# A hybrid DeltaNet layer on one core: reloads, squares and stores placed elsewhere in the queues, weight pairs dealt 18 and 14

## The chip, the cores and the metric

The kernel runs on one core of one Trainium2 chip. Its time is device microseconds of one execution; lower is better. Engines: TensorE (PE, with PEld for its weight loads), VectorE (DVE), ScalarE (ACT), GpSimd (POOL), and SyncE (SP), which only issues DMAs. ScalarE can issue DMAs too. Each engine works through its own list of instructions in order: an instruction that waits holds up all behind it.

## The reference

One layer on x of 2048 steps by 1024 features, all float32:

```python
h = rmsnorm(x, norm_in_w)
proj = h @ w_in            # 1024 -> 8208 columns
qkv, z_g, b_g, a_g, gate_b, gate_c, h_c, z_c = split(proj)
qkv = silu(causal_depthwise_conv(qkv, conv_qkv_w))      # 4 taps
o = gated_delta_rule_chunked(l2norm(q)/sqrt(128), l2norm(k), v, g, beta)   # 8 heads, state 128x128
o = rmsnorm(o, gdn_norm_w) * silu(z_g)
y_c = gate_b * (causal_depthwise_conv(gate_c * h_c, conv_w) + conv_b) * silu(z_c)   # 3 taps
return rmsnorm(x + concat(o, y_c) @ w_out, final_norm_w)
```

## The kernel before, in words

**Precision.** Every large product is done in float16 with both operands split in a high and a low part: three matmuls (high by high, high by low, low by high) stand for one. On top of that the input projection uses Strassen's scheme: two blocks of 512 steps against two blocks of 128 columns take 7 products instead of 8. So a *pair* of column blocks for one half of the steps (1024) is 7 products of 12 matmuls of 128 by 512, that is 84 matmuls `ps_d<-xop,g` (or `gr`).

**Pairs and stages.** There are 32 pairs of column blocks: `kq` and `vz` for each of 8 heads, `ca` and `cb` for each of 8 channel groups. Each is needed for both halves of the steps, 64 in all. `PLAN` (L26) deals them to four *stages*, four heads each: stage A has heads 0 to 3 on the first half, B the same on the second half, C heads 4 to 7 on the first half, D the same on the second. Entry (n, m) of a head puts n conv pairs between its `kq` and its `vz`, and m behind. Before, every stage has 16 pairs. Then comes stage E, the output projection. By the count of the matmuls, pair 0 starts at 32.4 us of the span, pair 1 at 104.9, stage B at 539.1, C at 991.3, D at 1403.6, E at 1780.6.

**Weights.** A pair's float32 columns come in two DMAs of 512 KB (`raw`, issued by SP, `fetcher`). `scales` squares both on ScalarE (`junk_sq<-raw`, 1.04 us each) to find a power of two as scale, `prepare_hi` makes the high parts on ScalarE (`g<-raw`, `g<-st`), `prepare_lo` the low ones on VectorE. Five results per pair (tags G1, G2, G7, G3, G4, one buffer each in stage A) are stored to DRAM (`wc<-g`, 512 or 256 KB); a buffer is written again only after its store has read it. In stage A the products read the `g` tiles at once, while the pairs of set one (`NA_` of them, 16) are split; in stages B and C set two is split meanwhile, and stages B, C and D load the split weights back (`gr<-wc`, SP). `raw` buffers: four in stage A, two later.

**Operands from x.** Seven tiles of 1 MB (`xop`) hold the split Strassen operands of one half; at the end of each stage they are loaded anew from `x0d` or `x1d` (`reload_x`, issued by ScalarE), each as soon as its last product of the stage is done. `later_x` makes `x1d` during stage A.

**Heads.** `gdn` runs beside the pairs: chunk matrices, an inversion on GpSimd (`nbx`, 31 steps), then a recurrence over 8 chunks, each a chain TensorE, VectorE, TensorE, ScalarE (`u<-ps_r`), TensorE, VectorE.

**Order.** All of these are Python generators. While the program is built, a model clock (`Clock`) gives every instruction a cost, and `do` hands an instruction out when the model says that its inputs are `lead` us away or past: 0 for ScalarE and VectorE, -2 for SP, `SAFE` = -4 for the squares (so, ready 4 us ago). A smaller number thus puts an instruction later in its queue, behind more work of its engine. The chip follows the order, not the model's times. On the chip every DMA, from whichever queue, uses one of 8 completion semaphores in turn, and the queue that issues it waits until the DMA eight places before it has landed (`DMAHW` in the built program).

**Evacuation.** ScalarE copies five of a pair's results out of PSUM (`c<-ps_d`); the products have four PSUM banks, so TensorE soon waits when ScalarE stands still.

Of the kernel before, what the change touches and what calls it, by code (L numbers as in the profile page):

```python
# [24 lines left out]
SAFE = -4.0  # L25
RATE = {"SP": 330e3, "ACT": 200e3}  # L26
PLAN = (((4, 0), (2, 0), (1, 0), (1, 0)), ((2, 0),) * 4, ((2, 0),) * 4, ((1, 0), (1, 0), (1, 1), (0, 4)))
# [204 lines left out]
def hybrid_layer_kernel(ctx, tc, x, norm_in_w, w_in, conv_qkv_w, A_log, dt_bias, gdn_norm_w,  # L232
# [10 lines left out]
    KT = KD // 2  # L243
# [189 lines left out]
    HH, GG = H // 2, G // 2  # L433
    for qt in range(4):
        grp, half = divmod(qt, 2)
        convs = [(f, half, grp * GG + g) for g in range(GG) for f in ("ca", "cb")]
        n0 = len(pairs)
        for i in range(HH):
            h = grp * HH + i
            order.append((half, h))  # L440
            pair("kq", half, h)
            if grp == 0 and i == 0:
                plan.append(("gates", half, 0, None))
            n, m = PLAN[qt][i]
            for c in convs[:n]:
                pair(*c)
            pair("vz", half, h)
            for c in convs[n:n + m]:
                pair(*c)
            convs = convs[n + m:]  # L450
        QOF += [qt] * (len(pairs) - n0)
        for p in range(n0, len(pairs)):
            if half == 0:
                WID.append(len(prep))
                prep.append(p)
            else:
                WID.append(WID[pairs.index((0,) + pairs[p][1:])])
# [155 lines left out]
    def first_x():  # L613
# [14 lines left out]
        def block0():  # L628
            for k in range(KD):
                pt = yield from acq("t")  # L630
                yield from trans(pt, k, 0)
                o = xop[X11 if k < KT else X21]
                yield from do(ACT.activation, kept(k), pt, AF.Copy, scale=sx_of(k))
                rel(pt)
                yield from split16(o[:, k % KT], kept(k))
                mark("x", 0, X11 if k < KT else X21, k % KT)

        def block1():
            for i in range(CB, 2 * CB):
                yield from norm_tile(xt0[i], junk[:, i % 2])  # L640
            for kt in range(KT):
# [6 lines left out]
                rel(pt)  # L648
                pt = yield from acq("t")
# [69 lines left out]
    def reload_x():  # L719
        yield from need(("x0d",))  # L720
        for qt in range(1, 4):
            for o in PRODUCTS:
                yield from need(("free", qt - 1, o))
                src = x1d[STORED.index(o)] if qt % 2 else x0d[o]
                xop[o] = hp.tile([P, KT, NR, 2, QW], F16, tag=f"X{o}", name="xop")
                yield from do(ACT.dma_start, xop[o].rearrange("p k r s w -> p (k r s w)"),
                              src.rearrange("p k r s w -> p (k r s w)"))
                for kt in range(KT):
                    mark("x", qt, o, kt)
# [10 lines left out]
    def scales():  # L740
        for p in range(NP):
# [5 lines left out]
            for j in range(2):  # L747
                yield from do(ACT.activation, junk_sq, raws[p, j].rearrange("p k c -> p (k c)"),
                              AF.Square, accum_out=ss[:, j:j + 1], lead=SAFE if p else None)
            pt = yield from acq("t")  # L750
            yield from do(PE.matmul, pt[:, 0:2], ones_b, ss.bitcast(BF16)[:, 1::2], start=True, stop=True,
                          lead=-3.0 if p else None)
# [30 lines left out]
    def prepare_lo():  # L783
        def keep(g, at, p, tag):
# [3 lines left out]
            yield from do((ACT if p < NA_ else SP).dma_start, wcd[p][:, at * WG:at * WG + n], g.rearrange("p s k c -> p (s k c)"))  # L788
# [356 lines left out]
    def gdn(half, h, st):  # L1145
# [160 lines left out]
        for b in range(2):  # L1306
            po = yield from acq("o")
            po = po.rearrange("p (c i) -> p c i", i=P)
            for i in range(CB):
# [7 lines left out]
                else:  # L1317
                    yield from do(PE.matmul, pa, kq(c)[:, 0, :], S, start=True, stop=True)
                    yield from do(DVE.scalar_tensor_tensor, r, pa, dec[:, 0, h, c:c + 1], vp[:, c, :],
                                  op0=ALU.mult, op1=ALU.subtract, back=9.0)  # L1320
                    yield from do(PE.matmul, po[:, i, :], S, kq(c)[:, 1, :], start=True, stop=False)
                yield from do(PE.matmul, pu, W[:, c, :], r, start=True, stop=True)
                u = sm.tile([P, P], F32, tag="u", name="u")
                yield from do(ACT.activation, u, pu, AF.Copy, back=9.0)
                yield from do(PE.matmul, pe, ksts[b][:, i, :], u, start=True, stop=True)
# [5 lines left out]
                yield from do(PE.matmul, po[:, i, :], u, NA(c)[:, 1, :], start=first, stop=True)  # L1331
# [251 lines left out]
    spawn(later_x(), 2)  # L1583
# [104 lines left out]
```

## Time and profile before

| | before |
|---|---|
| median of 3 runs | 2143.87 us (2138.94 to 2148.57) |
| the profiled execution | 2136.86 us, span 2135.1 us |
| mean granted TensorE clock | 0.957 of 2.4 GHz |
| TensorE busy | 1937.4 us, 91% |
| VectorE, ScalarE, GpSimd busy | 61%, 45%, 42% |

An engine's busy time is the union of its instructions. The clock is given as a share of the full 2.4 GHz; its lower level here is 0.5 (1.2 GHz). A time in brackets behind a row of the timeline is the idle time of that engine just before, with what ended it.

### The profile page before, as it was taken

To read this page: it belongs to the slowest core of one execution; us is meant where nothing else is said; L and a number is where in the kernel's file an instruction comes from. 1 tells how busy PE (TensorE), PEld (TensorE's weight loads), DVE (VectorE), ACT (ScalarE), POOL (GpSimd) and SP (SyncE) were. 2 spreads that over 40 slices of the span, in tenths; PEclk is the share of its full clock that TensorE was granted. 3 is DMA by queue.
4 is the path that set the end of the run, shared out by engine and by line. 5 is a ranking of instruction groups with operands and counts; after the bars stand their busy time and mean duration, and the time that the engine had idled before them with its cause. 6 is when DMAs were issued, how large, how long until landed. Compare 5 with 4: busy or idle time off the path is not lost. (4 is left out here: it accounts for less than half of the span.)

```text
span 2135.1 us, 30331 instructions
## 1 busy us (share of the span) xinstructions
PE 1937.4 (91%) x10832; PEld 1055.9 (49%) x10832; DVE 1307.1 (61%) x2437; ACT 968.5 (45%) x1884; POOL 899.5 (42%) x1441
## 2 busy tenths in 40 slices
PE   3696898787999989887999999999999999999998
PEld 1343354345555545444555555546656555444443
DVE  5785777866786656564758676655675754523321
ACT  5564565544554444343545555354544534423210
POOL 3446533745547373634463737245546261100000
PEclk9798899898999999998999999899999999999999
DMA  6357676775766786758676766585656668423110
GB/s 152 83 116 177 184 178 172 191 199 173 217 142 196 128 181 139 175 146 284 171 193 155 208 188 178 188 282 169 196 170 205 193 209 318 141 92 112 66 49 30
DMA packets 262381, 360.37 MB, mean 169 GB/s; under 512 B 67661, under 2 KB 180694, under 8 KB 258646
## 3 DMA queue, kind: packets, MB, share of 16 engines
q1 hardware_dynamic: 246678, 299.71, 53.3%
q10 hardware_dynamic: 15552, 58.73, 7.3%
q8 instruction: 85, 1.39, 0.3%
q14 instruction: 66, 0.54, 0.1%
HBM read 238.69 MB, written 119.67 MB: 168 GB/s over the span
## 5 line engine op out<-in xcount | busy, mean ns | idle before, releaser
L207 PE MATMUL ps_d<-xop,gr 128*128 128x512 f16 x4032 | 981.0, 384 | 21.5 <-DMA gr<-wc 11.6
L207 PEld LDWEIGHTS <-gr 128*128 128x128 f16 x4032 | 393.6, 99 | 394.2 <-DMA gr<-wc 20.2
L207 PE MATMUL ps_d<-xop,g 128*128 128x512 f16 x1344 | 338.9, 400 | 52.3 <-ACT c L207 12.8
L207 ACT ACTIVATE c<-ps_d 128x512 f32<-128x512 f32 x320 | 189.4, 592 | 329.5 <-PE ps_d L207 305.3
L207 PE MATMUL ps_d<-wo,mm 128*128 128x512 f16 x1536 | 335.5, 379 | 1.4 <-ACT mm L207 0.8
L207 POOL TENSOR_TENSOR nbt<-nbx,nb 128x60 f32<-128x60 f32 (+24 forms) x496 | 192.2, 387 | 140.3 <-DMA nb<-nd 103.9
L207 PEld LDWEIGHTS <-g 128*128 128x128 f16 x1344 | 134.5, 102 | 208.1 <-issue 56.5
L207 PEld LDWEIGHTS <-mm 128*128 128x128 f16 x1536 | 149.1, 98 | 176.7 <-ACT mm L207 1.0
L207 POOL TENSOR_TENSOR nbx<-nbx,nbt 128x60 f32<-128x60 f32 (+24 forms) x496 | 202.0, 407 | 37.2
L207 POOL TENSOR_TENSOR c<-c,c 128x512 f32<-128x512 f32 (+1 forms) x48 | 94.8, 1974 | 228.3 <-ACT c L207 142.7
L207 DVE SCALAR_TENSOR_TENSOR kq<-c,wq,kq 128x512 f32<-128x512 f32 x192 | 158.4, 829 | 6.5 <-ACT kq L207 2.3
L207 DVE SCALAR_TENSOR_TENSOR g<-raw,wsc,g 128x1024 f16<-128x1024 f32 (+1 forms) x96 | 114.2, 1193 | 32.8 <-ACT g L207 27.8
L207 DVE SCALAR_TENSOR_TENSOR res<-ps_d,msc,res 128x512 f32<-128x512 f32 x32 | 22.6, 747 | 173.8 <-PE ps_d L207 173.8
L207 POOL TENSOR_TENSOR p<-p,nhalf_pow 128x2 f32<-128x2 f32 (+1 forms) x51 | 37.8, 741 | 205.7 <-DVE p L207 185.5
L207 POOL TENSOR_TENSOR oss<-oss,nhalf_pow 128x16 f32<-128x16 f32 x32 | 99.3, 3103 | 59.1 <-DVE oss L207 58.8
L207 DVE TENSOR_TENSOR c<-ps_d,c 128x512 f32<-128x512 f32 x128 | 87.5, 684 | 48.3 <-PE ps_d L207 41.4
L207 DVE SCALAR_TENSOR_TENSOR S_all<-S_all,dec,ps_r 128x128 f32<-128x128 f32 x120 | 41.1, 342 | 122.7 <-PE ps_r L207 122.6
L207 POOL TENSOR_TENSOR stat<-stat,nhalf_pow 128x1 f32<-128x1 f32 x16 | 8.6, 538 | 252.9 <-DVE stat L207 252.9
L207 ACT ACTIVATE g<-raw,wsc 128x1024 f16<-128x1024 f32 (+1 forms) x96 | 95.4, 999 | 38.4 <-DVE wsc L207 25.3
L207 ACT ACTIVATE mm<-mr,msc 128x1024 f16<-128x1024 f32 x32 | 36.2, 1144 | 153.1 <-PE ps_d L207 134.6
L207 ACT ACTIVATE u<-ps_r 128x128 f32<-128x128 f32 x128 | 34.9, 273 | 147.8 <-PE ps_r L207 144.4
L207 PE MATMUL ps_r<-u,kst 128*128 128x128 f32 x256 | 54.0, 294 | 30.6 <-ACT u L207 30.6
(235 smaller groups left out, 2871.3 us busy)
## 6 DMA issues: line engine op xcount, KB each, us to landing
gr<-wc SPq DMA_DIRECT2D x144, 512.0 KB, 3.9
raw<-in_w_in_dram SPq DMA_DIRECT2D x64, 512.0 KB, 10.0
wc<-g ACTq DMA_DIRECT2D x32, 512.0 KB, 4.1
wc<-g SPq DMA_DIRECT2D x32, 512.0 KB, 3.8
wor<-in_w_out_dram SPq DMA_DIRECT2D x32, 512.0 KB, 5.2
mr<-mixd SPq DMA_DIRECT2D x32, 512.0 KB, 5.1
xop<-x1d ACTq DMA_DIRECT2D x14, 1024.0 KB, 8.7
wc<-g ACTq DMA_DIRECT2D x48, 256.0 KB, 4.4
```

The source lines that it names most:

```text
L207: return raw(*a, **k)
```

## The change

Six edits, all in what the builder decides; the arithmetic stays.

```diff
-SAFE = -4.0
-RATE = {"SP": 330e3, "ACT": 200e3}
-PLAN = (((4, 0), (2, 0), (1, 0), (1, 0)), ((2, 0),) * 4, ((2, 0),) * 4, ((1, 0), (1, 0), (1, 1), (0, 4)))
+SAFE = -6.0
+XL = -4.0
+RL = -0.4
+RATE = {"SP": 330e3, "ACT": 250e3}
+GA = 5
+PLAN = (((4, 0), (3, 0), (2, 0), (1, 0)), ((2, 0), (3, 0), (2, 0), (3, 0)),
+        ((1, 0), (2, 0), (1, 0), (2, 0)), ((0, 0), (1, 0), (1, 0), (0, 4)))
...
-        convs = [(f, half, grp * GG + g) for g in range(GG) for f in ("ca", "cb")]
+        convs = [(f, half, g) for g in (range(GA, G) if grp else range(GA)) for f in ("ca", "cb")]
...
+                mark("xk", k)
...
+                yield from need(("xk", kt), ("xk", kt + KT))
...
-                              src.rearrange("p k r s w -> p (k r s w)"))
+                              src.rearrange("p k r s w -> p (k r s w)"), lead=XL)
...
-                              AF.Square, accum_out=ss[:, j:j + 1], lead=SAFE if p else None)
+                              AF.Square, accum_out=ss[:, j:j + 1], lead=SAFE if p > 1 else None)
...
-                          lead=-3.0 if p else None)
+                          lead=-3.0 if p > 1 else None)
...
-            yield from do((ACT if p < NA_ else SP).dma_start, wcd[p][:, at * WG:at * WG + n], g.rearrange("p s k c -> p (s k c)"))
+            yield from do(SP.dma_start, wcd[p][:, at * WG:at * WG + n], g.rearrange("p s k c -> p (s k c)"))
...
-                    yield from do(PE.matmul, pa, kq(c)[:, 0, :], S, start=True, stop=True)
+                    yield from do(PE.matmul, pa, kq(c)[:, 0, :], S, start=True, stop=True, lead=RL)
...
-    spawn(later_x(), 2)
+    spawn(later_x(), 1)
```

`RL` goes to six matmuls of the recurrence and has the value that TensorE's default lead has. The first set now has five channel groups, 18 pairs, the second three, 14; so stages A and B have 18 pairs each, C and D 14. `RATE` of ScalarE's queue enters the model only. Built, both kernels have the same 5376 pair matmuls; DMAs fall from 1079 to 1071.

Stage A, ScalarE before, while pair 13 is multiplied (`wc_137`, `wc_138`: DRAM tiles of two pairs; `c_3597`: a pair's result):

```order
L207 DMA wc_137<-g 128x2048
L207 ACTIVATE vacc<-c_3335,wq 128x1024
L207 ACTIVATE g<-st,wsc 128x512 x2
L207 ACTIVATE c_3596<-ps_d 128x512
L207 DMA x0d<-xop 128x4096
L207 DMA wc_138<-g 128x1024
L207 ACTIVATE g<-raw,wsc 128x1024
L207 DMA wc_137<-g 128x1024
L207 ACTIVATE c_3597<-ps_d 128x512
L207 ACTIVATE junk_sq,wss<-raw 128x1024 x2
L207 ACTIVATE c_3597<-ps_d 128x512
```

The same part of stage A, SP after:

```order
L211 DMA wd<-nbx 256x1x32
L211 DMA wc_137<-g 128x1024
L211 DMA Wt_216<-wd 32x8x32 x4
L211 DMA wc_137<-g 128x2048
L211 DMA nd<-NA 32x4x32 x4
L211 DMA mixd<-c_2699 128x8x128
L211 DMA wc_138<-g 128x2048
L211 DMA wc_137<-g 128x1024
L211 DMA nd<-NA 32x4x32 x4
L211 DMA raw<-in_w_in_dram 128x8x128
L211 DMA wc_138<-g 128x1024
```

Four store issues between ScalarE's splits and evacuations are gone from its list; stores now alternate on SP with `raw` loads, and behind `wd<-nbx`, `Wt<-wd` and `nd<-NA`, which wait for GpSimd and VectorE.

Stage B, ScalarE before, where the weight pair with `raw_7765` is squared (numbers kept; `c1_7824`, `c2_7825`: pair 29's results):

```order
L207 ACTIVATE c1_7824<-ps_d_7826 128x512
L207 ACTIVATE kq_7833<-c2_7594,wq_7821 128x4x128
L207 ACT_TABLE_LOAD
L207 ACTIVATE E_7595<-E_7595,ngc_5031 128x128 x7
L207 ACTIVATE c2_7825<-ps_d_7826 128x512
L207 ACTIVATE junk_sq_157,wss_7801<-raw_7765 128x1024
L207 ACTIVATE junk_sq_157,wss_7801<-raw_7718 128x1024
L207 ACTIVATE oc_7921<-ps_o_7522 128x512
L207 ACTIVATE c2_7825<-ps_d_7902 128x512
```

ScalarE after, the weight pair of that place in its set, `raw_7229`:

```order
L211 ACTIVATE c1_7309<-ps_d_7311 128x512
L211 ACT_TABLE_LOAD
L211 ACTIVATE kq_7320<-kq_7320 128x4x128
L211 ACTIVATE kq_7320<-c2_7144,wq_7306 128x4x128
L211 ACTIVATE kq_7356<-kq_7356 128x4x128
L211 ACTIVATE c2_7310<-ps_d_7311 128x512
L211 ACTIVATE kq_7320<-kq_7320 128x4x128
L211 ACTIVATE junk_sq_157,wss_7255<-raw_7229 128x1024
L211 ACTIVATE junk_sq_157,wss_7255<-raw_7139 128x1024
L211 ACTIVATE junk_sq_157,kss_7323<-ps_t_7361 128x128
L211 ACTIVATE c2_7310<-ps_d_7393 128x512
```

The squares stand where they stood among a pair's evacuations; what moved is the distance to their load. In the order in which the builder hands out instructions, 55 pair matmuls lie between the issue of `raw_7765` and its square, and 84 between that of `raw_7229` and its square.

End of stage B, ScalarE before, the first reloads of `xop`:

```order
L207 DMA xop<-x0d 128x4096
L207 ACTIVATE u<-ps_r 128x128
L207 ACTIVATE sq<-sq 128x512
L207 DMA xop<-x0d 128x4096
L207 ACTIVATE sq<-sq 128x512
L207 DMA xop<-x0d 128x4096
L207 ACTIVATE c_8296<-ps_d 128x512
L207 ACTIVATE u<-ps_r 128x128
L207 ACTIVATE c_8296<-ps_d 128x512
L207 DMA xop<-x0d 128x4096
```

The same reloads after (`oc`, `osq`: a head's output):

```order
L211 DMA xop<-x0d 128x4096
L211 ACTIVATE c_8970<-ps_d 128x512
L211 DMA xop<-x0d 128x4096
L211 ACTIVATE c_8970<-ps_d 128x512
L211 DMA xop<-x0d 128x4096
L211 ACTIVATE g<-st,wsc 128x512 x2
L211 ACTIVATE c_8969<-ps_d 128x512
L211 DMA xop<-x0d 128x4096
L211 ACTIVATE oc<-ps_o 128x512
L211 ACTIVATE osq<-oc 128x512
L211 DMA xop<-x0d 128x4096
```

The second and the third reload now stand behind an evacuation each, where one `sq` stood, and there is no `u` of a recurrence between the reloads.

## Rows read from the trace of the kernel before

**Rows 1.** The page's first part: busy us, share of the span, instructions.

```profile
PE 1937.4 (91%) x10832; PEld 1055.9 (49%) x10832; DVE 1307.1 (61%) x2437; ACT 968.5 (45%) x1884; POOL 899.5 (42%) x1441
```

**Rows 2.** Busy us by stage: length, PE, PEld, DVE, ACT, POOL, clock, DMA share, GB/s.

```profile
104.90:539.10 434.20, 363.11 (x1909) 189.00 (x1909) 317.85 (x560) 237.13 (x453) 217.71 (x318) 0.92 0.68 176
539.10:991.30 452.20, 408.81 (x2431) 234.60 (x2429) 291.00 (x555) 204.20 (x414) 221.38 (x355) 0.96 0.72 172
991.30:1403.60 412.30, 391.85 (x2283) 222.38 (x2282) 280.25 (x521) 192.78 (x387) 216.39 (x369) 0.96 0.67 193
1403.60:1780.60 377.00, 376.05 (x2385) 220.75 (x2384) 241.32 (x436) 179.62 (x362) 172.41 (x308) 1.00 0.65 208
```

**Rows 3.** Timeline of ScalarE, stage B: squares, the idle time ahead in brackets.

```profile
751.05 1.06 ACT L207 ACTIVATE junk_sq<-raw 128x1024 bf16<-128x1024 f32 x1 [6.75 <-DMA raw<-in_w_in_dram]
...
802.32 1.06 ACT L207 ACTIVATE junk_sq<-raw 128x1024 bf16<-128x1024 f32 x1 [3.83 <-DMA raw<-in_w_in_dram]
...
862.80 1.06 ACT L207 ACTIVATE junk_sq<-raw 128x1024 bf16<-128x1024 f32 x1 [8.62 <-DMA raw<-in_w_in_dram]
...
915.77 1.06 ACT L207 ACTIVATE junk_sq<-raw 128x1024 bf16<-128x1024 f32 x1 [6.46 <-DMA raw<-in_w_in_dram]
```

**Rows 4.** Busy us by pair: seven with a stall, then one without.

```profile
728.30:763.30 35.00, 27.88 (x175) 17.34 (x174) 13.79 (x28) 12.27 (x24) 8.82 (x23) 0.95 0.97 181
785.60:814.60 29.00, 22.25 (x102) 10.86 (x102) 13.01 (x25) 15.32 (x34) 12.35 (x20) 0.88 0.80 176
840.90:875.00 34.10, 27.45 (x152) 17.27 (x150) 11.84 (x25) 11.55 (x23) 9.99 (x25) 0.90 0.90 183
899.30:927.80 28.50, 20.54 (x91) 9.12 (x90) 11.98 (x24) 15.31 (x35) 7.86 (x11) 0.88 0.78 162
956.10:991.10 35.00, 26.91 (x137) 16.95 (x135) 10.67 (x22) 9.42 (x20) 9.07 (x26) 0.85 0.92 279
991.30:1021.00 29.70, 25.75 (x124) 14.20 (x123) 19.19 (x30) 10.40 (x16) 21.55 (x44) 0.89 0.77 243
1362.50:1403.70 41.20, 34.53 (x157) 21.11 (x157) 13.23 (x30) 13.52 (x27) 25.22 (x70) 0.83 0.88 314
1216.90:1235.60 18.70, 18.70 (x91) 8.78 (x90) 14.52 (x29) 16.26 (x35) 6.64 (x4) 1.00 0.63 181
```

**Rows 5.** Timeline of ScalarE: what stood behind three reloads of x.

```profile
975.67 0.60 ACT L207 ACTIVATE c<-ps_d 128x512 f32<-128x512 f32 x1 [9.77 <-DMA gr<-wc]
...
997.26 1.15 ACT L207 ACTIVATE c<-c,wsc 128x1024 f32<-128x1024 f32 x1 [5.48 <-DMA gr<-wc]
...
1404.15 1.15 ACT L207 ACTIVATE c<-c,wsc 128x1024 f32<-128x1024 f32 x1 [6.14 <-PE ps_d L207]
```

**Rows 6.** DMA issues (count, KB, us to landing): A, late B, C; then the page's reloads.

```profile
raw<-in_w_in_dram SPq DMA_DIRECT2D x26, 512.0 KB, 9.3
...
raw<-in_w_in_dram SPq DMA_DIRECT2D x8, 512.0 KB, 15.3
...
raw<-in_w_in_dram SPq DMA_DIRECT2D x12, 512.0 KB, 10.0
...
xop<-x1d ACTq DMA_DIRECT2D x14, 1024.0 KB, 8.7
```

**Rows 7.** Stores of split weights on ScalarE: issue ns min/median/max, first and last.

```profile
L207 ACTq DMA_DIRECT2D wc<-g x80: 325/326/3188, 33.7 to 531.8; - x80
```

**Rows 8.** Timeline of ScalarE, stage A: a split that waited behind two stores' issues.

```profile
445.57 1.15 ACT L207 ACTIVATE g<-raw,wsc 128x1024 f16<-128x1024 f32 x1 [5.70 <-DMA nd<-NA]
```

**Rows 9.** Waits of SP's queue, 100 to 540 us: us in total, times, longest.

```profile
SPq L207 <- DVE NA L207: 36.0, 4, 17.5
...
SPq L207 <- POOL nbx L207: 29.8, 2, 18.2
...
SPq L207 <- ACT o L207: 22.1, 2, 21.5
...
SPq L207 <- POOL xc L207: 20.7, 1, 20.7
```

More of the change, by code (lines that the diff above doesn't have):

```diff
@@ L432, in hybrid_layer_kernel @@
     order, QOF, WID, prep = [], [], [], []
-    HH, GG = H // 2, G // 2
+    HH = H // 2
     for qt in range(4):
         grp, half = divmod(qt, 2)
-        convs = [(f, half, grp * GG + g) for g in range(GG) for f in ("ca", "cb")]
+        convs = [(f, half, g) for g in (range(GA, G) if grp else range(GA)) for f in ("ca", "cb")]
         n0 = len(pairs)
@@ L1317, in gdn @@
                 else:
-                    yield from do(PE.matmul, pa, kq(c)[:, 0, :], S, start=True, stop=True)
+                    yield from do(PE.matmul, pa, kq(c)[:, 0, :], S, start=True, stop=True, lead=RL)
                     yield from do(DVE.scalar_tensor_tensor, r, pa, dec[:, 0, h, c:c + 1], vp[:, c, :],
                                   op0=ALU.mult, op1=ALU.subtract, back=9.0)
-                    yield from do(PE.matmul, po[:, i, :], S, kq(c)[:, 1, :], start=True, stop=False)
-                yield from do(PE.matmul, pu, W[:, c, :], r, start=True, stop=True)
+                    yield from do(PE.matmul, po[:, i, :], S, kq(c)[:, 1, :], start=True, stop=False, lead=RL)
+                yield from do(PE.matmul, pu, W[:, c, :], r, start=True, stop=True, lead=RL)
                 u = sm.tile([P, P], F32, tag="u", name="u")
                 yield from do(ACT.activation, u, pu, AF.Copy, back=9.0)
-                yield from do(PE.matmul, pe, ksts[b][:, i, :], u, start=True, stop=True)
+                yield from do(PE.matmul, pe, ksts[b][:, i, :], u, start=True, stop=True, lead=RL)
                 if first:
@@ L1330, in gdn @@
                                   op0=ALU.mult, op1=ALU.add, back=9.0)
-                yield from do(PE.matmul, po[:, i, :], u, NA(c)[:, 1, :], start=first, stop=True)
+                yield from do(PE.matmul, po[:, i, :], u, NA(c)[:, 1, :], start=first, stop=True, lead=RL)
                 rel(pr)
```

## The prediction

> **What bounds the kernel now.** I read the page's first part, then a table of busy time by stage, then who ends TensorE's waits in each stage, then the timelines of the engines named there. The page shows one engine near its limit: TensorE is busy 91% of the span, the next one, VectorE, 61% [rows 1]. So time can only come from places where TensorE stands still or runs at its lower clock. I call *lost* what remains of a stretch when TensorE's busy time, multiplied by the granted clock, is taken off. From the table by stage [rows 2]: stage A from pair 1 on, 434.2 - 363.1 x 0.92 = 100.1 us; B, 452.2 - 408.8 x 0.96 = 59.7; C, 412.3 - 391.9 x 0.96 = 36.1; D, 377.0 - 376.05 = 1.0. D shows what the kernel can do: the same pairs and heads without a loss. The reader is to see that A, B and C are not bound by work on TensorE, and that D is.
>
> In B the timeline of ScalarE names the cause. Four times it stands at the first square of a weight pair and waits for the load of `raw`: 6.75, 3.83, 8.62 and 6.46 us [rows 3], 25.7 us together. Evacuations and the recurrence's copies stand behind. The four pairs in which this happens (the first four of [rows 4]) lose 8.5, 9.4, 9.4 and 10.4 us, 37.7 together; a pair without a stall loses nothing (18.70 us long, all of it busy, clock 1.00). The loss is above the wait because TensorE, idle for several microseconds, then goes on at the lower of its clock levels for a while: the granted clock is 0.88 to 0.95 in these pairs.
>
> At the ends of B and C the cause is a reload of x in ScalarE's queue [rows 5]: behind three of them the next instruction came 9.77, 5.48 and 6.14 us late, the first two released by the landing of another DMA (the one eight places before, on the same completion semaphore), the third by TensorE. The pairs there (the next three of [rows 4]) lose 12.1, 6.8 and 12.5 us, 31.4 together.
>
> Stage A is of another kind. Its 100.1 us lie in many short waits over 15 pairs, 6.7 us a pair, while VectorE is busy 317.9 of 434.2 us and ScalarE 237.1 [rows 2]: the splitting of weights, with one buffer for each result, is what TensorE waits for.
>
> **The change part by part.** *Squares.* In B a pair matmul costs 392.5 / (16 x 84) = 0.292 us without losses [rows 2]. Counted in built order, 33, 55, 39 and 55 pair matmuls lay between the later `raw` issue and the square in the four stalled places; after the change the same four weight pairs of set two have 41, 77, 43 and 84. That is 2.3, 6.4, 1.2 and 8.5 us more. If the loads land as late after their issue as before, waits of 4.4, 0, 7.4 and 0 us are left, and in proportion losses of 5.5 and 8.1. So 24.1 of 37.7 us go. Bounds: 37.7, if loads land sooner (set two has 14 pairs beside 18 multiplied, less DMA work per pair), and nothing, if the load slips with the rest of SP's queue.
>
> *Reloads.* The reload behind which 9.77 us were lost stood 26 pair matmuls behind the DMA whose landing it needed; now it is 49, 6.7 us more. At the other two places a lead of 4 us takes 4 of 5.48 and 4 of 6.14. In proportion to the losses that is 8.3 + 5.0 + 8.1 = 21.4 of 31.4 us. What it costs: the first use comes sooner after the reload. It was 62 to 73 pair matmuls away at the ends of B and C, now it is 37 to 62; 37 are 10.8 us, and a reload takes 8.7 us to land in the median [rows 6]. That cover is thin. Were three tiles as late as loads late in B, 15.3 us [rows 6], they would cost 3 x 4.5 = 13.5 us. So the bounds are a gain of 31.4 and a loss of 13.5.
>
> *Stores.* 80 store issues leave ScalarE, at least 0.326 us each: 26.1 us [rows 7]. Some of them also made ScalarE wait for SP's DMAs, as the split that came 5.70 us late behind two issues shows [rows 8]. TensorE gains where ScalarE was next in its chain; I take ScalarE's busy share of stage A, 237.1 / 434.2 = 55%, of 26.1 us: 14.3. On SP now 90 stores stand in line, and there waits of others are ahead of them: four for chunk matrices (`DVE NA`), two for the inversion (`nbx`), two for `ACT o`, one for `POOL xc`, the longest of each kind 17.5 to 21.5 us [rows 9]. A store that is late holds its buffer, ScalarE's next split of that tag waits, and with it TensorE. I put nothing for it into the sum, because SP's lead of -2 us lets most stores be ready, and keep the price for a rival: 9.4 us for each such hit (a stalled pair of B, [rows 4]), nine at most, 85 us. The other bound is a gain of 26.1 us plus a few waits, 30.
>
> The Trainium skill, "DMA: Bandwidth & Descriptors", section "Issuing engines are not separate DMA queues", says that DMAs from all engines run on the same 16 DMA engines and that issuing from several saves only the sequencer's issue time, usually small. By that rule the move is worth at most the 26.1 us; the 5.70 us of [rows 8] speak for more, since there the issuer waited.
>
> *18 and 14 pairs.* A and B get two pairs more, C and D two less; TensorE's work only moves. What changes is the loss that goes with a pair: in A 2 x 6.7 = +13.3 us; in B, without the stalls above, (59.7 - 37.7 - 12.1) / 16 = 0.6, so +1.2; in C (36.1 - 6.8 - 12.5) / 16 = 1.05, so -2.1. D has its heads closer together (two pairs between the first two), which nothing in this trace shows at that density: 0 to two stalls of 9.4; I take 3, near the D of before. For A the bounds are 0, if the extra pairs fill waits, and 2 x (434.2 / 15 - 18.7) = 20.5, if each is as long as A's mean with no head work to share it. `RL` equals the default lead of TensorE, the last head of D keeps its four conv pairs behind it, and the later priority of `later_x` and the wait for `xk` move work inside A only: nothing.
>
> *Sum.* -24.1 - 21.4 - 14.3 + 13.3 + 1.2 - 2.1 + 3 = -44.4 us. The profiled execution took 2136.86 us (span 2135.1), so it would take 2092.5. The median of the runs shown is 7.0 us above that execution; the same step from 2143.87 gives 2099.5, and I predict 2100.
>
> **Rivals.** *Stores behind SP's waits (slower).* For it: SP's long waits in stage A are there [rows 9], and stores must be read out before five single buffers are written again. Against: in B and C 80 stores go through SP already, and apart from the seven stalls the pairs there lose only 0.6 and 1.05 us each. Each hit costs 9.4 us, so the fifth of nine eats the gain of 44.4; all nine give +41, 2185.
>
> *Loads slip too (no change).* If squares and reloads come later but their loads slip by as much, since SP's queue is in order and now longer, those two gains are nothing: -14.3 + 13.3 + 1.2 - 2.1 + 3 = +1.1, 2145. For it: the same 512 KB took 9.3 us to land in A, 10.0 in C and 15.3 late in B [rows 6], so the load and not the order may be the cause. Against: the distances grew in all four places.
>
> *One ring for loads and stores (no change).* In A, with stores on ScalarE's queue, loads land in 9.3 us; late in B, with stores on SP's, in 15.3 [rows 6]. If that is the reason (C, with stores on SP too and loads of 10.0 us, speaks against it), squares in A begin to stall as they did in B. With a quarter of 18 weight pairs stalled at 9.4 us it costs 42, and the time is 2142. The Trainium skill, "DMA: Bandwidth & Descriptors", section "Queues, rings and completion order", states such a rule: a DMA engine takes turns between the queues that have work, so a load on a queue of its own gets turns beside stores, and one behind stores in the same queue does not. By that rule loads in A land later; the trace agrees for late B and not for C.
>
> *Everything goes (faster).* With the upper bounds, -37.7 - 31.4 - 26.1 + 13.3 + 1.2 - 2.1 + 3 = -79.8: 2064. For it: D lost only 1.0 us of 377 [rows 2].
>
> **How the numbers follow.** About 0.5%, 10.7 us, is what a measurement of this kernel can tell from no change: faster is below 2133.2, slower above 2154.6. The forecast has 0.57 (its own range, 2075 to 2130), everything goes 0.08, the two that end near no change 0.08 and 0.08, stores behind SP 0.19. So faster has 0.57 + 0.08 and 0.01 from the lower edge of the two near no change, same 0.15, slower 0.19. The unknown costs reach from 2064 to 2185; leaving out a tenth at each end, the range is 2062 to 2165: above it lies a bit more than half of the slow case, below it little more than the end of the fast one.
>
> **What would show it.** Right: in B the brackets ahead of `junk_sq<-raw` shrink to two of 4 to 7 us; nothing above 5 us behind a reload at the ends of B and C; the lost time of B below 25 us, of C below 25; A near 114 us behind pair 1 with two pairs more; no `wc<-g` on ScalarE's queue. Wrong: TensorE waits for `xop<-x0d` at the start of C; `g<-raw` or `g<-st` on ScalarE released by `wc<-g`; `raw` landing in more than 13 us in A; a loss above 10 us in D. The prediction falls if A's loss grows by more than 45 us, or if the four waits of [rows 3] return at full length.

## The result, and the profile after

The changed kernel took 2118.48 us (median of 4, 2114.29 to 2119.7), the kernel before 2142.72 in the same runs: a ratio of 0.9881, with a 95% interval of 0.9854 to 0.9908. It is faster by 1.2%; 2.0% was predicted, and the time lies inside the range. The profiled execution took 2117.82 us, its span 2116.1, 19.0 less than before. How the time came about is another matter: most terms of the sum were wrong, and that the time lies inside the range is in large part luck.

The page's first part after, columns as in [rows 1]:

```profile
PE 1920.0 (91%) x10832; PEld 1048.1 (50%) x10832; DVE 1292.6 (61%) x2450; ACT 974.9 (46%) x1881; POOL 877.3 (41%) x1433
```

Busy time by stage after, the rows that answer to [rows 2]: pair 0, A, B, C, D, E.

```profile
32.90:100.80 67.90, 45.52 (x189) 23.16 (x190) 54.89 (x83) 41.97 (x74) 34.11 (x30) 0.77 0.34 87
100.80:576.90 476.10, 408.80 (x2180) 212.89 (x2180) 343.21 (x635) 266.29 (x503) 237.86 (x336) 0.94 0.67 173
576.90:1054.90 478.00, 434.27 (x2526) 243.34 (x2524) 303.94 (x563) 210.37 (x409) 229.61 (x390) 0.96 0.71 170
1054.90:1402.30 347.40, 331.74 (x2036) 191.04 (x2035) 233.57 (x451) 168.39 (x345) 163.99 (x298) 0.98 0.72 204
1402.30:1752.10 349.80, 341.45 (x2146) 205.68 (x2146) 232.02 (x432) 172.98 (x350) 172.64 (x319) 1.00 0.64 204
1752.10:2116.10 364.00, 352.34 (x1747) 168.73 (x1747) 113.00 (x246) 98.57 (x175) 29.10 (x37) 0.98 0.31 107
```

The same view of the kernel before, for pair 0 and stage E, which were not shown:

```profile
32.40:104.90 72.50, 48.00 (x189) 24.73 (x190) 52.99 (x83) 43.59 (x76) 33.37 (x28) 0.74 0.32 81
...
1780.60:2135.10 354.50, 343.69 (x1629) 161.18 (x1627) 111.72 (x244) 95.00 (x167) 28.28 (x36) 1.00 0.30 102
```

Lost time (length less busy time by clock), against the prediction's terms put to their stages:

| stage | predicted | before, after | measured |
|---|---|---|---|
| pair 0 | 0 | 37.0, 32.8 | -4.2 |
| A | -14.3 + 13.3 = -1.0 | 100.1, 91.8 | -8.3 |
| B | -24.1 - 8.3 + 1.2 = -31.2 | 59.7, 61.1 | +1.4 |
| C | -5.0 - 8.1 - 2.1 = -15.2 | 36.1, 22.3 | -13.8 |
| D | +3 | 1.0, 8.4 | +7.4 |
| E | 0 | 10.8, 18.7 | +7.9 |
| sum | -44.4 | | -9.6 |

The span fell by 19.0. The other 9.4 us are in TensorE's busy time by clock; two digits of the clock leave about 2 us of doubt in each long stage, and I assign them to nothing. What the reader is to see: B, where 31 us were to go, lost as much as before.

Where B's time went is on VectorE's timeline, stage B (in brackets the idle time ahead of the instruction and what ended it):

```profile
803.85 0.69 DVE L211 TENSOR_TENSOR kq<-qe,kq 128x512 f32<-128x512 f32 x1 [11.41 <-DMA qe<-gd]
...
918.01 0.69 DVE L211 TENSOR_TENSOR kq<-qe,kq 128x512 f32<-128x512 f32 x1 [11.85 <-DMA qe<-gd]
```

And on ScalarE's, the one square of B that still waits long, and the instruction behind a reload of x at the start of C:

```profile
916.69 1.06 ACT L211 ACTIVATE junk_sq<-raw 128x1024 bf16<-128x1024 f32 x1 [6.95 <-DMA raw<-in_w_in_dram]
...
1070.55 1.06 ACT L211 ACTIVATE vacc<-vacc 128x1024 f32<-128x1024 f32 x1 [10.07 <-DMA wd<-nbx]
```

Of the four waits in [rows 3], 25.7 us, one of 6.95 is left. But the load `qe<-gd` (512 KB for a head) stands behind the same loads of `raw` in SP's queue, and VectorE now waits for it where ScalarE had waited for `raw`; the recurrence's `S_all` and `r` stand behind. The reload's wait of [rows 5] is still there, 10.07 us.

Why are those loads late? Landing of `raw` in A and in B (count, KB, median us), then of five weight pairs of B, two loads each: `ca` of group 5, `vz` of head 4, `kq` and `vz` of head 5, `kq` of head 6.

```profile
raw<-in_w_in_dram SPq DMA_DIRECT2D x30, 512.0 KB, 8.5
raw<-in_w_in_dram SPq DMA_DIRECT2D x16, 512.0 KB, 15.5
...
raw<-in_w_in_dram SPq DMA_DIRECT2D x2, 512.0 KB, 15.6
raw<-in_w_in_dram SPq DMA_DIRECT2D x2, 512.0 KB, 10.2
raw<-in_w_in_dram SPq DMA_DIRECT2D x2, 512.0 KB, 15.5
raw<-in_w_in_dram SPq DMA_DIRECT2D x2, 512.0 KB, 16.6
raw<-in_w_in_dram SPq DMA_DIRECT2D x2, 512.0 KB, 11.2
```

The weights are loaded in blocks of 128 columns, which I number 0 to 7 within each 1024. Slow are the blocks with number 5 (of group 5 or head 5), and in the old order the four stalls of [rows 3] were `kq`, `ca`, `cb` and `vz` of number 5 too. So not the stage nor the queue seems to matter but the columns. While the first of the two loads of `vz` of head 5 runs (issued at 885.8, landed at 901.3 us; the second was issued at 899.0 and landed 17.7 us later), the DMA engines are nearly full and move little (queue, packets, MB, share of 16 engines):

```profile
q1 hardware_dynamic: 1424, 1.15, 91.3%
```

That is 0.913 x 16 x 15.5 / 1424 = 0.159 us for a packet of mostly 512 bytes.

### The profile page after: what moved, and what is told of

Read it like the earlier page. It is cut to its first block, busy times and chain, and to the rows that moved or that the text cites. A ratio compares the mean times of both kernels' runs of the same rounds, so it can differ in the third digit from the quotient of the medians.

```text
span 2116.1 us, 30380 instructions
## 1 busy us (share of the span) xinstructions
PE 1920.0 (91%) x10832; PEld 1048.1 (50%) x10832; DVE 1292.6 (61%) x2450; ACT 974.9 (46%) x1881; POOL 877.3 (41%) x1433
## 4 chain that ended last, share of the span: by engine, by line
PE 59%; DMA 12%; DVE 10%; POOL 9%; issue 5%; ACT 3%; SPq 1%; POOLq 0%; DVEq 0%; ACTq 0%
PE ps_d L211 48%; PE ps_t L211 6%; POOL nbt L211 3%; POOL nbx L211 3%; PE ps_r L211 3%; DMA qe<-gd 3%; DVE g L211 2%; DMA wc<-g 2%; PE ps_o L211 2%; SPq L211 1%; DMA raw<-in_w_in_dram 1%; DMA gr<-wc 1%; DVE kq L211 1%; DVE c L211 1%; ACT junk_sq L211 1%
## 5 line engine op out<-in xcount | busy, mean ns | idle before, releaser
L211 PE MATMUL ps_d<-xop,gr 128*128 128x512 f16 x3864 | 940.0, 383 | 13.8 <-ACT c L211 6.8
L211 PEld LDWEIGHTS <-gr 128*128 128x128 f16 x3864 | 376.6, 99 | 369.3 <-issue 22.9
L211 PE MATMUL ps_d<-xop,g 128*128 128x512 f16 x1512 | 380.1, 398 | 67.1 <-ACT g L211 27.7
L211 PEld LDWEIGHTS <-g 128*128 128x128 f16 x1512 | 148.9, 102 | 239.4 <-issue 46.2
L211 POOL TENSOR_TENSOR nbt<-nbx,nb 128x60 f32<-128x60 f32 (+24 forms) x496 | 198.0, 399 | 148.3 <-DMA nb<-nd 112.2
L211 POOL TENSOR_TENSOR nbx<-nbx,nbt 128x60 f32<-128x60 f32 (+24 forms) x496 | 193.6, 390 | 36.7
L211 POOL TENSOR_TENSOR c<-c,c 128x512 f32<-128x512 f32 (+1 forms) x36 | 68.5, 1901 | 124.5 <-ACT c L211 75.3
L211 ACT ACTIVATE g<-raw,wsc 128x1024 f16<-128x1024 f32 (+1 forms) x96 | 95.3, 998 | 31.2 <-DVE wsc L211 22.4
L211 DVE SCALAR_TENSOR_TENSOR r<-ps_r,dec,vp 128x128 f32<-128x128 f32 x120 | 41.6, 346 | 95.4 <-PE ps_r L211 95.1
L211 ACT ACTIVATE mm<-mr,msc 128x1024 f16<-128x1024 f32 x32 | 36.1, 1144 | 133.5 <-PE ps_d L211 120.3
```

Source lines behind the costliest of these rows:

```text
L211: return raw(*a, **k)
```

## The experiments

Each edits the changed kernel, except `plan_back_soon`, which edits `plan_back`, and two programs that only load. Ratios are to the kernel before in the same runs; the changed kernel itself has 0.9881 [0.9854, 0.9908].

| run | median us | ratio, 95% interval |
|---|---|---|
| block5_first | 2113.49 | 0.9868 [0.9828, 0.9907] |
| stores_back | 2105.55 | 0.9826 [0.9785, 0.9867] |
| reload_lead_0 | 2121.76 | 0.9907 [0.9877, 0.9937] |
| squares_back | 2120.55 | 0.9893 [0.9871, 0.9915] |
| qe_on_scalar | 2099.73 | 0.9799 [0.9775, 0.9824] |
| plan_back | 2138.41 | 0.9980 [0.9964, 0.9995] |
| plan_back_soon | 2102.25 | 0.9816 [0.9790, 0.9842] |
| plan_20_12 | 2155.17 | 1.0059 [1.0041, 1.0076] |
| qe_and_stores | 2102.58 | 0.9802 [0.9777, 0.9827] |
| late_only_block5 | 2095.14 | 0.9783 [0.9769, 0.9797] |

Any edit makes the builder deal out a new order everywhere, and two orders that differ in nothing of interest can be some microseconds apart: below, the stores' edit, which touches only A, shortens E by 11 us, and the reloads' edit takes B's loss from 61.1 to 45.5. So I rest on stages and waits as well as on totals. Losses in the expectations that differ from the table's by up to 2 us (A 93.7, B 59.2, D 10.0) were worked out with more digits of the clock.

**Is it the columns?** `loads_alone` has no layer at all:

```python
for base in (q, k, v, z, conv parts):            # starts of 8 x 128 columns
    for i in range(8):
        nc.sync.dma_start(one, w[:, :, base + i * 128: base + i * 128 + 128])
```

> Leaves out the whole layer: it only loads column blocks of w_in (128 columns, 512 KB, 1024 rows of 512 bytes 32,832 bytes apart), one at a time into one buffer, all eight blocks of q, k, v, z and of two conv parts in order, then block 2 and block 5 of q in other shapes (by eight DMAs of 128 rows; as two halves of 64 columns; as 256 columns; with rows dealt to partitions in another order). Theory (column block): in both traces the weight pairs of column block 5 (four of the second set) have packets of 105 to 154 ns in the median where others have 27, whenever they are loaded; so here every sixth of eight loads takes 12 to 17 us and the others 5 to 8. Rival (queue): the load is late because of stores and reloads on the same queue; then all 48 loads take the same within 1 us.

The last eight loads (us to landing, columns 0 to 7 in order); the first of them still ran beside the end of a store, the others alone:

```profile
oneraw<-in_w_in_dram SPq DMA_DIRECT2D x1, 512.0 KB, 10.7
oneraw<-in_w_in_dram SPq DMA_DIRECT2D x1, 512.0 KB, 7.5
oneraw<-in_w_in_dram SPq DMA_DIRECT2D x1, 512.0 KB, 6.6
oneraw<-in_w_in_dram SPq DMA_DIRECT2D x1, 512.0 KB, 5.8
oneraw<-in_w_in_dram SPq DMA_DIRECT2D x1, 512.0 KB, 7.2
oneraw<-in_w_in_dram SPq DMA_DIRECT2D x1, 512.0 KB, 4.9
oneraw<-in_w_in_dram SPq DMA_DIRECT2D x1, 512.0 KB, 6.1
oneraw<-in_w_in_dram SPq DMA_DIRECT2D x1, 512.0 KB, 8.4
```

The same shape takes 4.9 to 8.4 us alone and 10.7 where it is slow, and the first of eight was slow in each of the six parts (10.7 to 14.3); the next run has it alone, with 12.6. The rival, one value for all 48, falls. But here number 0 is slow and 5 the fastest: which one it is differs between programs. In the layer it is number 5 in all twelve traces: the packets of 512 bytes that move around the two loads of a weight pair take 94 to 190 ns in the mean for number 5, 36 to 98 for the others.

`shapes_alone` loads the first 1024 columns in other shapes, each load after the one before.

> Leaves out the whole layer: loads of the first 1024 columns of w_in only, each waiting for the one before. In the first run of loads alone one block of eight was slow (10.7 to 13.7 us behind the first one, the fastest block 4.9 to 6.5), another block than in the layer's kernel. Theory (the rows of one block, 32,832 bytes apart, fall on few places of the memory at once): with rows p*8+k dealt to partition p, so that other rows are read at the same time, the slow block is another one or none is over 9 us; two blocks in one load cost less than the two alone; two queues for one block don't help, since the place is the limit: 10 us or more for the slow one. Rival (the block's addresses are slow whatever the order): the same block is slow in every shape. Rival (one queue is the limit): two queues halve the time of every block.

Number 0 took 12.6 us (others 5.9 to 8.8), with rows dealt p*8+k 11.5 (5.3 to 7.8), and half of its rows, with the other half on ScalarE's queue, 9.7 (3.7 to 4.8). So the same block stays slow in another order of the rows, against my theory, and two queues don't cure it. Two blocks in one load of 1 KB rows took 11.5 where number 0 is one of them (7.4 to 8.6 else): the slow one costs 3 to 4 us there in place of 5 or more. What the queue did while number 0 was loaded alone:

```profile
q1 hardware_dynamic: 1040, 0.52, 17.2%
```

That is 0.172 x 16 x 12.6 / 1040 = 0.033 us a packet, with the DMA engines 17% busy; in the layer it was 0.159 us and 91%. That number 0 here and number 5 in the layer are slow for one reason is therefore not shown.

**Does the slowness move with the columns in the layer?**

```diff
+HEADS = (0, 5, 2, 3, 4, 1, 6, 7)
+CG = (0, 1, 2, 3, 5, 4, 6, 7)
-        convs = [(f, half, g) for g in (range(GA, G) if grp else range(GA)) ...]
+        convs = [(f, half, g) for g in (CG[GA:] if grp else CG[:GA]) ...]
-            h = grp * HH + i
+            h = HEADS[grp * HH + i]
```

> The changed kernel with heads 1 and 5 and channel groups 4 and 5 exchanged, so the four weight pairs of column block 5 are split in stage A (four raw buffers) and not in B. Theory (column block): in B the two waits of VectorE for qe<-gd (11.4 and 11.9 us) and the wait of the square (6.9) are gone and raw lands in 9 to 12 us in place of 15.5; the lost time of B falls from 61 to 30 or 40 us; A pays 0 to 20 for it; 2085 to 2112 us, forecast 2098. Rival (queue): B as before with waits of 7 to 12 us in other names, 2112 to 2125.

Stages A and B, and landing of `raw` in B:

```profile
101.10:593.00 491.90, 410.96 (x2180) 214.46 (x2180) 342.72 (x635) 266.15 (x503) 237.24 (x332) 0.93 0.71 166
593.00:1052.90 459.90, 434.47 (x2526) 243.45 (x2524) 302.79 (x563) 210.16 (x409) 231.93 (x393) 0.97 0.67 177
```

```profile
raw<-in_w_in_dram SPq DMA_DIRECT2D x16, 512.0 KB, 11.4
```

VectorE's waits for `qe` in B are 13.8 us in four, the longest 6.0. B lost 459.9 - 434.47 x 0.97 = 38.5 us in place of 61.1, A 109.7 in place of 91.8: the loss went the way the columns went, 22.6 out of B and 17.9 into A, and the total hardly moved: 2113.49 lies in the rival's range and above the theory's. Three of the four slow weight pairs show a landing in A, of 13.9 to 14.5 us, and B has no long wait behind one. So the place is shown. The size is not: in the other six runs with 18 pairs in B, where the columns stayed, B lost 42.5 to 53.9, so only 4 to 15 of the 22.6 us (an estimate from these runs) are surely the columns'. Counted another way, TensorE's idle time between the first issue of a slow weight pair and 12 us behind its second landing (16 us taken where no landing is recorded, so an estimate) is 32.3 of its 43.5 idle us of B in the changed kernel, 28.4 of 43.2 before, and none of 25.2 here; the idle time that lies elsewhere in B grew from 11.2 to 25.2.

**The squares, and who waits instead.** `squares_back` undoes the squares' edit.

```diff
-SAFE = -6.0
+SAFE = -4.0
-... lead=SAFE if p > 1 else None      # and the matmul behind, -3.0 if p > 1
+... lead=SAFE if p else None
```

> The changed kernel with SAFE -4 and the squares of the second weight pair early again. The prediction's term was 24.1 us: 2142. From the trace of the changed kernel (B loses 59.2 us, before 60.4) the wait only moved from the squares to qe<-gd behind the same slow loads: 2112 to 2126, with waits of 4 to 9 us ahead of junk_sq<-raw at the pairs of column block 5 and shorter ones of VectorE for qe.

Same time, as expected from the trace and not from the prediction. Five waits ahead of `junk_sq<-raw`, 30.2 us, the longest 9.12, are back in B; VectorE's and GpSimd's for `qe` fall from 44.4 to 26.0 us in all, with one of 11.32 left, and B loses 472.9 - 438.19 x 0.96 = 52.2, still less than the changed kernel. Pair 0 takes 71.5 us (72.5 before, 67.9 after): the early square of the second weight pair was worth 3.6 us, which I had put at nothing.

`qe_on_scalar` takes `qe` out of SP's queue.

```diff
-        yield from do(SP.dma_start, qe, gd[1, h:h + 1]...)
+        yield from do(ACT.dma_start, qe, gd[1, h:h + 1]...)
```

> The changed kernel with the 16 loads qe<-gd issued by ScalarE instead of SP, so they don't stand behind loads of raw in SP's queue. Theory (they are late because of 1 MB of slow packets ahead in the same queue): they land in under 9 us, VectorE's waits of 11.4 and 11.9 us in B fall under 4, the lost time of B falls from 59 to 40 or 45: 2098 to 2108. Rival (the 16 DMA engines, busy 0.93 to 0.98 in these stretches with packets of 130 ns, are the limit for every queue): landing over 12 us and 2112 to 2124.

Landing of `qe<-gd` over the whole program, the changed kernel and then this one:

```profile
DMA to landing us min/median/max: 5.1/7.4/16.8
```

```profile
DMA to landing us min/median/max: 3.3/6.2/8.6
```

The waits for `qe` fall from 44.4 to 13.0 us in all, and the kernel is 0.8% faster. B itself gained less than expected (472.6 - 438.33 x 0.96 = 51.8 lost): squares wait there again for `raw`, 17.8 us in three, and TensorE 12.7 us for `gr<-wc`, the longest 9.8. The other stages moved too: A lost 4.4 us less, D 3.6, E 5.0, C 7.2 more.

Was it the place in SP's queue that made `qe` late? This run can't tell: the two loads of `qe` in question are issued, in its new order, 23.5 and 22.3 us behind the last load of a slow weight pair, after that had landed. In two runs further down, `late_only_block5` and `qe_and_stores`, a load of `qe` on ScalarE's queue is issued 4.0 and 8.2 us behind a slow load that is still under way. VectorE then waits for it, and goes on 13.4 and 13.6 us behind the issue:

```profile
893.63 0.69 DVE L212 TENSOR_TENSOR kq<-qe,kq 128x512 f32<-128x512 f32 x1 [5.60 <-DMA qe<-gd]
...
795.42 0.69 DVE L211 TENSOR_TENSOR kq<-qe,kq 128x512 f32<-128x512 f32 x1 [7.08 <-DMA qe<-gd]
```

What moved in the first microseconds of these loads, 880.3 to 888 in the one and 781.8 to 788 in the other (`q1` is SP's queue, `q10` ScalarE's):

```profile
q1 hardware_dynamic: 641, 0.33, 95.6%
...
q1 hardware_dynamic: 706, 0.39, 76.9%
q10 hardware_dynamic: 27, 0.10, 3.9%
```

In the first run not one packet of ScalarE's queue moved for 7.7 us, with the DMA engines 96% busy on SP's. On SP's queue, 1.2 and 2.2 us behind a slow load, `qe` had taken 16.5 and 16.8 us in the changed kernel. So the rival fits better: the DMA engines, full of slow packets, hold up every queue, and a queue of its own is worth some 3 us at most (an estimate from these four loads). The Trainium skill, "DMA: Bandwidth & Descriptors", section "Queues, rings and completion order", says that a DMA engine takes turns between the queues it has work for, a packet at a time; the trace shows no such turn for those 7.7 us and few in the other run; why was not found out. The section "Issuing engines are not separate DMA queues" of that page of the Trainium skill says that issuing from several engines saves only the time of issuing; these two late loads agree. By this estimate most of the 18.7 us of this run come with its new order, in which `qe` missed the slow loads.

**The stores.**

```diff
-            yield from do(SP.dma_start, wcd[p]...)
+            yield from do((ACT if p < NA_ else SP).dma_start, wcd[p]...)
```

> The changed kernel with the 90 stores of the first set issued by ScalarE again. The prediction's term was 14.3 us: 2133. If only the issue time counts where ScalarE is next in the chain of a stage that still loses 92 us, 0 to 14: 2118 to 2133. Rival (the stores on SP hold up loads behind them and the saving is given back): 2118 or less, down to 2105. In the trace the wait of ScalarE for wc<-g and the issues of 0.33 us come back.

```profile
100.50:573.50 473.00, 403.14 (x2182) 210.61 (x2180) 355.01 (x634) 270.62 (x509) 249.45 (x342) 0.94 0.67 173
573.50:1046.50 473.00, 432.04 (x2521) 241.06 (x2522) 302.12 (x569) 205.64 (x405) 228.63 (x381) 0.97 0.74 178
```

A loses 473.0 - 403.14 x 0.94 = 94.0 us with the stores on ScalarE, 91.8 without: no difference. The issues come back in A (78 of 0.327 us, 25.5 us in all) and cost TensorE nothing that can be seen. The whole is 13 us faster than the changed kernel (by the two intervals together, 1 to 22): A is 3 us shorter, B 5, E 11, C and D together 7 longer. Why was not settled. The rival's total came true, but not by its sign: the waits of ScalarE's splits for a store (`wc<-g`) in A fell from 6.2 us in three, the longest 3.0, to 1.5 in one.

**The reloads.**

```diff
-XL = -4.0
+XL = 0.0
```

> The changed kernel with the reloads of x handed out at lead 0 again. The prediction's term was 21.4 us: 2140. From the trace of the changed kernel the start of C still has a wait of 9.7 us at a reload, so a smaller gain, 5 to 15: 2123 to 2133. Rival (the place of a reload is set by its buffer and its semaphore, not by the lead): 2112 to 2124.

No difference in the total. B, D and E:

```profile
572.60:1040.80 468.20, 435.78 (x2529) 243.38 (x2528) 293.99 (x554) 207.59 (x408) 235.10 (x395) 0.97 0.74 179
...
1387.30:1733.00 345.70, 340.23 (x2142) 204.25 (x2141) 227.72 (x426) 165.99 (x344) 158.03 (x320) 1.00 0.64 205
1733.00:2118.10 385.10, 360.50 (x1751) 170.98 (x1749) 121.04 (x262) 100.52 (x177) 33.11 (x39) 0.95 0.30 104
```

The pairs end at 1733.0, 19.1 us sooner than in the changed kernel, and E takes 21.1 us longer: TensorE waits 10.8 us there for the first tiles of `mm`, and for some time goes on partly at the lower clock level (granted clock 0.71 between 1745 and 1760 us). B and C lose 45.5 and 18.1 us in place of 61.1 and 22.3, so a gain of 20 us there is given back in E; which part of either belongs to the reloads was not settled. At the start of C the longest wait of ScalarE at a reload is 2.5 us, with the very lead that I had held responsible for 10.

**The plan.** `plan_back` has 16 pairs in every stage and keeps all other edits.

```diff
-GA = 5
-PLAN = (((4, 0), (3, 0), (2, 0), (1, 0)), ((2, 0), (3, 0), (2, 0), (3, 0)), ...
+GA = 4
+PLAN = (((4, 0), (2, 0), (1, 0), (1, 0)), ((2, 0),) * 4, ((2, 0),) * 4, ((1, 0), (1, 0), (1, 1), (0, 4)))
```

> The changed kernel with 16 pairs in every stage again (old PLAN, four channel groups in each set). By the prediction's terms (13.3 + 1.2 - 2.1 + 3 = 15.4 us as the cost of 18 and 14) it is faster: 2103. From the trace, stage A lost 93.7 us with 17 pairs behind pair 0, where it had lost 101.1 with 15, and D 10.0 in place of 0.9: then the loss doesn't go with the count of pairs, A loses 85 to 100 again, and the time is 2112 to 2130.

Stages A, B and C; TensorE's longest wait in the last 48 us of C (us in all, times, longest); SP there:

```profile
99.80:537.70 437.90, 366.93 (x1983) 189.77 (x1983) 312.58 (x591) 245.02 (x471) 224.28 (x324) 0.94 0.68 176
537.70:958.00 420.30, 398.52 (x2383) 229.68 (x2382) 283.56 (x546) 195.39 (x390) 211.46 (x383) 0.97 0.75 175
958.00:1402.00 444.00, 385.50 (x2255) 215.21 (x2254) 278.79 (x517) 199.10 (x392) 202.93 (x333) 0.94 0.68 193
```

```profile
PE ps_d L210 <- DMA gr<-wc: 29.7, 3, 13.5
```

```profile
1385.99 0.50 SPq L210 DMA_DIRECT2D wc<-g  x1
...
1394.84 1.75 SPq L210 DMA_DIRECT2D gr<-wc  x4
```

Without the plan the other five edits bring 0.2%: beside them the plan makes the gain, 20 us, and I had booked it as a cost of 15.4. A loses 93.0 us with 15 pairs behind pair 0 and 91.8 with 17, so its loss does not go with the number of pairs. What goes is in C: 81.6 lost with 16 pairs, 22.3 with 14 (B the other way, 33.7 and 61.1; with 16, the last of the four slow weight pairs falls into C, where its square waits 12.56 us). The rows say why. The weight pairs of set two are split one after the other, some 53 us each (not 48, as I had written), and the last of 16 is stored at 1386 while its pair begins at 1348; TensorE waits for the loads behind the last stores (11.4 of the 29.7 us behind the last one of all). Counted the same way (issue of the last store, first matmul of its pair), that room is -26 us in the kernel before, -38 in `plan_back`, +38 in the changed kernel.

`plan_back_soon` tests the room: 16 pairs again, but each weight pair squared sooner.

```diff
-SAFE = -6.0
+SAFE = -2.0
```

> plan_back (16 pairs in every stage, all other edits of the change kept) with SAFE -2 instead of -6, so that each weight pair of set two is squared and split some 4 us sooner. Theory (room): 16 weight pairs one after the other gain up to 64 us, the last store comes before its pair starts, and the waits for gr<-wc at the end of C (29.7 us in plan_back) fall under 10; C loses 40 to 55 in place of 80.7; in B waits ahead of junk_sq<-raw of 5 to 10 us come back: 2115 to 2132, forecast 2124. Rival (C's loss in plan_back comes from something else, reloads or heads): C still over 65, 2135 to 2150.

```profile
524.70:983.00 458.30, 418.26 (x2489) 238.69 (x2488) 299.77 (x559) 201.41 (x404) 216.10 (x361) 0.94 0.73 173
983.00:1366.00 383.00, 375.15 (x2273) 216.16 (x2272) 267.07 (x509) 189.22 (x380) 194.08 (x345) 0.99 0.72 203
```

C loses 11.6 us in place of 81.6, the room is -5 us, and no wait for `gr<-wc` is left at the end of C; B loses 65.1 in place of 33.7. B and C together lose 76.7 in place of 115.3: a part of C's loss, that of the slow square, only moved to B. The total is 36 us better than `plan_back`, more than I had expected, and better than the changed kernel itself, without its plan. So 18 and 14 pairs and a smaller delay are two ways to more room, and the larger delay of the change had used some of it up. The plan's 20 us are its worth beside that delay; beside the smaller one it was not measured.

`plan_20_12` goes on in the change's direction: `GA = 6`, 20 and 12 pairs.

> The changed kernel with 20 pairs in A and B and 12 in C and D (six channel groups in the first set). Theory (room): the weight pairs of set two are split one after the other, about 48 us each, and the plan helps because the last of them is ready before its pair is multiplied (its last store stood 26 us behind that start before, 38 us behind in plan_back, 38 us ahead in the changed kernel). With 12 there is over 100 us of room, but the changed kernel had no wait left there, so nothing more is won in C; D has its heads closer together and loses more than the 10.0 us of the changed kernel: 2112 to 2140, forecast 2122. Rival (the loss simply goes down with pairs moved to A and B): another 20 us, 2098.

It is slower than the kernel before. The room is 153 us and buys nothing; C loses 38.1 us, D 332.2 - 313.57 x 0.98 = 24.9, E 32.2, all three more than in the changed kernel. The direction was as expected; the size lies outside what was expected (2112 to 2140), and why C and E lose more was not found out.

**Put together.** `qe_and_stores` joins the two single edits that were faster.

> The changed kernel with both edits that made it faster alone: qe<-gd issued by ScalarE (2099.7 alone) and the stores of the first set back on ScalarE (2105.5 alone). If they act in different places (qe in stage B, stores at the end and in B), some of both: 2085 to 2097. If both only took load off SP's queue, or if each builds another order with other waits of its own, no more than the better one: 2097 to 2106.

They do not add up: 2102.58, as either alone. `late_only_block5` has `qe` on ScalarE and delays only the squares of the slow columns:

```diff
-... lead=SAFE if p > 1 else None)
+... lead=(SLOW if pairs[prep[p]][2] == 5 else SAFE) if p > 1 else None)     # SAFE -2, SLOW -8
```

> The changed kernel with qe<-gd issued by ScalarE and with the squares' lead by what the loads showed: -8 for weight pairs of column block 5 (loads of 15 to 18 us), -2 for all others. Theory (slow block and room): the squares of block 5 wait less than in plan_back_soon (8.7 and 8.5 us), the others don't take room (the last store 60 us or more ahead of its pair, no wait for gr<-wc at the end of C), qe keeps landing in under 9 us; B loses 30 to 45 in place of 52.9 with qe alone: 2080 to 2096, forecast 2089. Rival (another order brings other waits of the same size, as in qe_and_stores): 2096 to 2106.

```profile
571.00:1036.20 465.20, 437.70 (x2538) 246.12 (x2537) 304.22 (x578) 208.10 (x408) 226.33 (x388) 0.96 0.73 175
```

B loses 45.0 us, at the edge of what was expected; the room is 44 us, not 60; the squares of block 5 wait 7.9 us in all; `qe` did not keep under 9 us (10.7 at most among the landings recorded, 13.4 to VectorE's start above). With 2095.14 us it is the fastest of all, 23 us below the changed kernel, but its lead over `qe_on_scalar` is within the intervals.

## Why the prediction was right, and which steps failed

- *Squares, -24.1.* The distance did what the step said: 18.7 of 25.7 us of waiting are gone. The step that failed is "in proportion losses": it took the waiting engine for the cause. While the loads of a slow weight pair run, the DMA engines are nearly full of slow packets (91% for the load shown), and whatever comes next in the built order waits, `qe` or `gr` in place of the square; B lost as much as before. "Loads slip too" had the loads as the cause, but not that other engines would wait for them.
- *Reloads, -21.4.* Wrong in its cause. The wait of 10 us at the start of C stayed in spite of the lead. It ended with the landing of `wd<-nbx`, which SP had issued at 1054.34, among the reloads, and which took 15.8 us to land; in that time the DMA engines were full (the shares of the two queues add up to 99.9%). With the lead undone it was gone. The third wait of [rows 5], 6.14 us, was ended by TensorE, so a lead of the reload could not have shortened it. Of the 12.5 us at the end of C [rows 4], 3.6 us of TensorE's idle time were waits for `gr<-wc`, which are missing room and gone in the changed kernel (29.7 in `plan_back`); the rest stays open.
- *Stores, -14.3.* Measured 2 us in A. The step that failed is ScalarE's busy share of 55% as the chance that TensorE waits for an issue: the issues came back at no cost that the stage's sum shows. The rival in which stores on SP cost time is nearer in the total, since the kernel is faster with them back. Its hits in A are there but small: ScalarE's splits waited 6.2 us in all for `wc<-g` in the changed kernel.
- *18 and 14 pairs, +15.4.* The step that failed most: it took the loss of a stage as so much a pair. Measured -20 us beside the other edits; A gained two pairs at no loss, and C's loss fell by the end of a chain that I had not drawn, load, square, split, store, reload.
- *D, +3.* Mis-sized: D +7.4 and E +7.9, less than the bound of 18.8 for D alone.
- *Pair 0*, 4 us, was not in the sum.

So the predicted time was 18 us too low, and that the measured one lies inside the range is largely luck. Of the 19.0 us by which the span fell, pair 0 (4.2) and TensorE's busy time (9.4) stand under no term; the 31 us of B did not come; A gained 8 where 1 was put; only C came out near its term, and for another reason. Of the signs of being right, the brackets in B, C's loss and the stores' queue came out as said; B's loss (61.1, not under 25), A's (91.8, not 114) and the reload at the start of C (10.07, not under 5) did not. Of the signs of being wrong, two were there in small: TensorE waited 2.7 us for `xop<-x0d` at the start of C, and splits in A waited for `wc<-g`; D's loss (8.4 by the rows, 10.0 with more digits) stands at its bound. Of the rivals, "one ring" had named late loads behind others in one queue, but gave the stores as their cause; A's loads landed in 8.5 us with stores on the same queue.

## What to carry to other kernels

When an engine waits for a load, ask first why the load is late and what else is to be loaded in that time: to delay the one that waits can hand the wait to the next. For work that is prepared one piece after the other, compute the room between the last piece's end and its first use; a delay per piece is paid as often as there are pieces. A queue of its own did not get an urgent load past a slow one here; issuing it at another time did.

## What the runs showed of the hardware

A load of 1024 rows of 512 bytes, 32,832 bytes apart, took 4.9 to 8.8 us with nothing beside it, and 12.6 for one block of columns in eight. In the layer the loads of one block in eight took 13.9 to 21.1 us in the traces looked at, against some 9 to 11, with about 0.16 us for a packet where the slow load alone had 0.033. Another order of the rows or a second queue did not help the load alone, and a load on another queue beside a slow one in the layer was late too (13.4 and 13.6 us). Which columns are slow differed between programs; why was not found out, and neither whether it is the same slowness alone and in the layer.
